# Feed-forward blocks of a hybrid transformer layer: where the norm's steps, the sums of x and the first loads stand

## The chip, the cores and the metric

One NeuronCore of a Trainium2 chip runs the whole program. Its engines work from their own queues, each in order: PE (TensorE, the matrix products; PEld is its loading of weights), DVE (VectorE), ACT (ScalarE), POOL (GpSimd) and SP, which here issues every DMA. They meet through semaphores. The metric is the device time of one execution in microseconds, as a median over runs.

## The reference

One layer over 512 tokens of width 1024: a feed-forward block, an attention mixer, a second feed-forward block, and a last norm. What the change touches is the first part of both feed-forward blocks.

```python
def rmsnorm(x, g):
    xf = x.astype(jnp.float32)
    y = xf * lax.rsqrt(jnp.mean(xf * xf, axis=-1, keepdims=True) + NORM_EPS)
    return (y * g.astype(jnp.float32)).astype(x.dtype)

def swiglu(x, w_in, w_out):
    gate, up = jnp.split(x @ w_in, 2, axis=-1)
    return (jax.nn.silu(gate) * up) @ w_out
...
        h = h + 0.5 * swiglu(rmsnorm(h, ffn1_norm[l]), ffn1_w_in[l], ffn1_w_out[l])
        h = h + hybrid_mixer(...)
        h = h + 0.5 * swiglu(rmsnorm(h, ffn2_norm[l]), ffn2_w_in[l], ffn2_w_out[l])
    return rmsnorm(h, final_norm)
```

`w_in` is 1024 x 5632, `w_out` 2816 x 1024.

## The kernel before

The state `h` lies transposed in SBUF: 8 blocks of 128 rows (the width) by 512 columns (the tokens). Every operand of a product is split into a high part (a rounded copy, made by ACT) and a low part (the rest, made by DVE), and a product is three matmuls: high by high, high by low, low by high (`mm3_steps`, L205 to L211, for 512 columns; `product`, L300 to L308, for 256). `parts` (L159 to L164) makes the two parts of a block of x times the norm's gain; the division by the root of the mean square is left out of the operands and multiplied into the results later (`gated`).

A feed-forward block is `ffn`. Its 22 column blocks of `w_in` (128 gates and 128 ups each) come in two kinds:

- the first three are **plain blocks**: two products of 24 matmuls of 512 columns each, one for the gates and one for the ups, six products in all. Their weights are read by SP into pieces (`load_next`, L110) and split by `to_parts` (L97 on ACT, L98 on DVE).
- the other 19 are computed in quarters by a scheme of seven products of 12 matmuls of 256 columns (a Strassen-like scheme), which uses sums of quarters of x (`sums_of_x`) and sums of quarters of the weights (`sums_of_w`, a loop that makes them one block ahead: L274, L278, L284 the sums on DVE, L276, L282, L288, L293 the high parts on ACT, L279, L285, L290, L295 the low parts on DVE). The seven products of a block are issued in the order B11, T1, T2, B21, B22, T3 and (after the next block's B11) T4. The products by `w_out` (`out_steps`) are pushed in between.

Before the scheme can start, the work that stands beside the plain blocks must be done: the **norm** (squares of h on ACT, L168 and L171, added up on DVE, L172; `rstd_col`: a product of the sum with ones on PE, L185, a root on ACT, L187, with a table load before it, a reciprocal on DVE, L189; `rstd_bc`: a product with the identity that spreads the result over the partitions, L196, copied by ACT, L200), the **sums of x** (scaled copies of h on ACT, L231; sums on DVE, L239, L240, L243, L244; their high parts on ACT, L247, and low parts on DVE, L248), the **gating** of the three plain blocks (L333, L337, L339 on DVE, the Silu on ACT, L335, the parts of the result, L326 and L328), and the first block's sums of w.

Order: the program is written as one stream, and generators (`side_step`) take a step of the sums of x or w at every second step of a product. A scheduler then lays each engine's queue down, and it can move an instruction ahead of its place in the text; it is fixed when the program is built. In the first feed-forward block the first two products run side by side while x and the weights are still loading (`two`, `steps`).

Tiles: `u` holds operands (32 buffers), `tmp` 128x512 scratch (10), `t8`/`t` raw weights (4 of 1 MB), `sm` the gains, `acc` the sum of squares; `mm`, `sc` and `pv` are PSUM banks (4, 3 and 1).

## Time and profile before

| | |
|---|---|
| median of 3 runs | 1008.36 us (1007.68 to 1011.56) |
| the profiled execution, its own time | 1003.63 us |
| its span | 1001.7 us |
| mean granted clock of TensorE in it | 0.991 |
| PE busy | 972.7 us (97%), 6196 matmuls |
| DVE, ACT busy | 802.5 us (80%), 511.4 us (51%) |
| DMA | 93.59 MB, mean 93 GB/s |

How to read it: the span is what the rows add up to; the time of the execution is 1.9 us longer. PE is busy nearly all the time, so the question is where it is not, and where it runs slowly. A row of the timeline gives the start, the duration, the engine, the line, the operation, what it writes and reads, and in brackets how long its engine had been idle and what it waited for. Matmuls overlap: the pitch from one start to the next tells the rate, not the duration of one.

### The profile page before, as it was taken

The page shows a single profiled execution, that of the slowest core. Times are in us where ns is not written, and L with a number is a line of the kernel's source. Part 1 is how long each engine was busy: PE and PEld are TensorE (multiplying, and loading weights), DVE is VectorE, ACT ScalarE, POOL GpSimd, SP SyncE. Part 2 cuts the span into 40 slices and gives each one's busy share as a digit, 9 for nine tenths or more (in the row PEclk, how much of TensorE's full clock was granted, in tenths as well). Part 3 has the DMA queues.
Part 4 walks back from the last instruction along what each step waited for, and adds up shares of the span by engine and source line. Part 5 has one row for each costly group of instructions (what it writes and reads, how often), then busy time and mean ns, then how long its engine had stood idle before and what let it go on. Part 6 is the DMA issues. An engine that isn't in the chain of part 4 may idle for free.

```text
span 1001.7 us, 15923 instructions
## 1 busy us (share of the span) xinstructions
PE 972.7 (97%) x6196; PEld 869.0 (87%) x6196; DVE 802.5 (80%) x1466; ACT 511.4 (51%) x1037; POOL 0.2 (0%) x4
## 2 busy tenths in 40 slices
PE   7899999999999999999999999979999999999996
PEld 5699999999999889888777888859999999999996
DVE  7699868788696675787899899789977878779665
ACT  8454344443444355554777786745534435344344
POOL 0000000000000000000000000000000000000000
PEclk9999999999999999999999999989999999999998
DMA  7233223122224313123311113114331323313112
GB/s 297 64 127 116 90 101 137 74 106 88 102 86 141 124 37 111 43 78 98 128 43 45 41 43 106 43 43 147 116 130 60 137 74 106 126 64 96 43 43 84
DMA packets 36506, 93.59 MB, mean 93 GB/s; under 512 B 4432, under 2 KB 8912, under 8 KB 36432
## 3 DMA queue, kind: packets, MB, share of 16 engines
q1 hardware_dynamic: 36432, 92.59, 26.8%
q8 instruction: 48, 0.79, 0.3%
q14 instruction: 26, 0.21, 0.1%
HBM read 88.87 MB, written 2.10 MB: 91 GB/s over the span
## 4 chain that ended last, share of the span: by engine, by line
PE 93%; DVE 3%; ACT 2%; issue 1%; DMA 1%; SPq 0%; DVEq 0%; ACTq 0%
PE mm L306 9%; PE mm L307 9%; PE mm L308 9%; PE sc L210 9%; PE sc L209 9%; PE sc L208 9%; PE mm L208 5%; PE mm L210 5%; PE mm L209 5%; PE sc L308 4%; PE sc L307 4%; PE sc L306 4%; PE mm L855 2%; PE pv L892 2%; PE pv L893 2%; PE mm L711 1%
## 5 line engine op out<-in xcount | busy, mean ns | idle before, releaser
L306 PE MATMUL mm<-u 128*128 128x256 f32 x760 | 214.9, 283 | 0.2 <-ACT u L282 0.2
L307 PE MATMUL mm<-u 128*128 128x256 f32 x760 | 215.0, 283 | 0.0
L308 PE MATMUL mm<-u 128*128 128x256 f32 x760 | 215.0, 283 | 0.0
L208 PE MATMUL sc<-u 128*128 128x512 f32 (+1 forms) x400 | 156.3, 391 | 7.7 <-ACT u L97 7.0
L210 PE MATMUL sc<-u 128*128 128x512 f32 (+1 forms) x400 | 155.0, 387 | 2.4 <-DVE u L98 2.4
L209 PE MATMUL sc<-u 128*128 128x512 f32 (+1 forms) x400 | 155.5, 389 | 0.0
L306 PEld LDWEIGHTS mm<-u 128*128 128x128 f32 x760 | 144.8, 191 | 7.6 <-DVE tmp L514 0.5
L307 PEld LDWEIGHTS mm<-u 128*128 128x128 f32 x760 | 145.1, 191 | 5.6
L308 PEld LDWEIGHTS mm<-u 128*128 128x128 f32 x760 | 145.0, 191 | 0.5
L208 PE MATMUL mm<-u 128*128 128x512 f32 (+1 forms) x248 | 98.8, 398 | 2.7 <-ACT u L97 2.7
L210 PE MATMUL mm<-u 128*128 128x512 f32 (+1 forms) x248 | 95.6, 386 | 0.1
L209 PE MATMUL mm<-u 128*128 128x512 f32 (+1 forms) x248 | 95.1, 383 | 0.0
L210 PEld LDWEIGHTS sc<-u 128*128 128x128 f32 x400 | 76.5, 191 | 20.3 <-DVE u L98 3.0
L306 PE MATMUL sc<-u 128*128 128x256 f32 x304 | 86.6, 285 | 5.2 <-ACT u L276 5.2
L208 PEld LDWEIGHTS sc<-u 128*128 128x128 f32 x400 | 77.3, 193 | 15.4 <-ACT u L97 7.4
L308 PE MATMUL sc<-u 128*128 128x256 f32 x304 | 86.6, 285 | 0.0
L307 PE MATMUL sc<-u 128*128 128x256 f32 x304 | 86.5, 285 | 0.0
L209 PEld LDWEIGHTS sc<-u 128*128 128x128 f32 x400 | 77.3, 193 | 6.5
L358 ACT CAST u<-tmp 128x512 fp32r<-128x512 f32 (+1 forms) x96 | 54.6, 582 | 43.9 <-PE sc L210 21.0
L381 DVE SCALAR_TENSOR_TENSOR h<-sc,h 128x512 f32<-128x512 f32 x85 | 58.4, 687 | 11.9 <-PE sc L210 11.8
L359 DVE TENSOR_TENSOR u<-tmp,u 128x512 fp32r<-128x512 f32 (+1 forms) x96 | 60.9, 641 | 8.5 <-ACT u L358 8.3
L306 PEld LDWEIGHTS sc<-u 128*128 128x128 f32 x304 | 58.5, 192 | 8.0 <-ACT u L276 5.4
(223 smaller groups left out, 1948.9 us busy)
## 6 DMA issues: line engine op xcount, KB each, us to landing
t<-in_f_wi_dram SPq DMA_DIRECT2D x86, 512.0 KB, 4.3
tmp<-in_f_wo_dram SPq DMA_DIRECT2D x80, 256.0 KB, 4.8
t<-in_wm_t_dram SPq DMA_DIRECT2D x13, 512.0 KB, 4.3
t<-in_cw_dram SPq DMA_DIRECT2D x8, 512.0 KB, 4.9
tmp<-in_f_wo_dram SPq DMA_DIRECT2D x16, 128.0 KB, 3.8
t<-in_wm_oa_dram SPq DMA_DIRECT2D x4, 512.0 KB, 3.9
out_dram<-tmp SPq DMA_DIRECT2D x8, 256.0 KB, 2.1
t<-in_wm_n_dram SPq DMA_DIRECT2D x4, 408.0 KB, 3.6
```

The lines of the kernel that those rows point to most:

```text
L208: PE.matmul(o, wh[:, c], xs[k][:, 0, :], start=s0, stop=False)
L209: PE.matmul(o, wh[:, c], xs[k][:, 1, :], start=False, stop=False)
L210: PE.matmul(o, wl[:, c], xs[k][:, 0, :], start=False, stop=s1)
L306: PE.matmul(o, w[0][:, c], x[k][0], start=new, stop=False, skip_group_check=not first)
L307: PE.matmul(o, w[0][:, c], x[k][1], start=False, stop=False, skip_group_check=not first)
L308: PE.matmul(o, w[1][:, c], x[k][0], start=False, stop=k == 3, skip_group_check=not first)
L358: A.copy(u[:, 0, :n], raw[:, :n])
L359: V.tensor_tensor(u[:, 1, :n], raw[:, :n], f(u[:, 0, :n]), op=ALU.subtract)
L381: V.scalar_tensor_tensor(h[:, i, :], o, 0.5, h[:, i, :], op0=ALU.mult, op1=ALU.add)
L855: PE.transpose(pt[:rows, r * P : (r + 1) * P], pl[r][:, cols], ident)
L892: PE.matmul(pv, v, u[:, 0, :], start=a, stop=False)
L893: PE.matmul(pv, v, u[:, 1, :], start=False, stop=b)
```

## The change

It has five parts, all in `ffn`'s plain blocks and in the program's first microseconds.

1. **First loads.** The table of gains is loaded first; the first two blocks of x come in one DMA (rows of 4 KB in place of 2 KB), and so does each of the first two pieces of weights, which were read in halves. Seven DMAs stand ahead of the identity's in place of ten; the rest of x follows in pairs of blocks as before.
2. **Products of ones.** Eight 128x128 products of a tile of ones (`wake`, L92) are issued on PE while these loads run. Nothing reads their result.
3. **Root's table.** ACT's first activation is a root (`late`, L88), so that the table for roots is loaded at the start; the load ahead of the norm's root in the first block is gone.
4. **Squares.** In the first block, the squares of h take their bias from `late`, which is written (as zero) after the last block of x is split. This orders them behind the splitting of x; four come after the first two products, the others at steps of the third.
5. **Norm's steps and sums of x.** In the first block the norm's product with ones stands after the third step of the fourth product, and the product with the identity after the second step of the fifth; in the second block after the fourth step of the first and the second step of the second. Before, the text had them between products. The sums of x are made in lots: scaled copies, sums, high parts and low parts of successive lots overlap by one, where before each lot was finished before the next was begun.

In the first two products the two are now advanced two steps at a time in turn, in place of one.

The diff, cut to its core:

```diff
--- before.py
+++ after.py
@@ -76,14 +76,20 @@
 
     h = sb.tile([P, KB, 512], F32, tag="h", name="h")
     sm = sb.tile([P, S_W], F32, tag="sm", name="sm")
-    nc.sync.dma_start(h[:, 0:1, :], xT[:, 0:1, :])
     nc.sync.dma_start(sm, small)
-
+    nc.sync.dma_start(h[:, 0:2, :], xT[:, 0:2, :])
+
+    epsc = sb.tile([P, 1], F32, tag="epsc", name="epsc")
+    V.memset(epsc, EPS)
     ones = sb.tile([P, P], F32, tag="ones", name="ones")
     V.memset(ones, 1.0)
-    epsc = sb.tile([P, 1], F32, tag="epsc", name="epsc")
-    V.memset(epsc, EPS)
-    A.copy(epsc, epsc)
+
+    late = sb.tile([P, 1], F32, tag="late", name="late")
+    A.activation(late, epsc, AF.Sqrt)
+
+    wake = ps("pv")
+    for _ in range(8):
+        PE.matmul(wake[:, :P], ones, ones, start=True, stop=True)
     ident = sb.tile([P, P], F32, tag="ident", name="ident")
     rowm = sb.tile([P, 1], F32, tag="rowm", name="rowm")
 
@@ -163,12 +169,12 @@
         A.activation(u[:, 0, :], h[:, k, :], AF.Copy, scale=gc)
         V.scalar_tensor_tensor(u[:, 1, :], h[:, k, :], gc, f(u[:, 0, :]), op0=ALU.mult, op1=ALU.subtract)
 
-    def squares(k, acc):
+    def squares(k, acc, zero=0.0):
         if k == 0:
-            A.activation(acc, h[:, k, :], AF.Square)
+            A.activation(acc, h[:, k, :], AF.Square, bias=zero)
         else:
             sq = tmp()
-            A.activation(sq, h[:, k, :], AF.Square)
+            A.activation(sq, h[:, k, :], AF.Square, bias=zero)
             V.tensor_tensor(acc, acc, sq, op=ALU.add)
 
     def feed(k, gcol, xs, acc):
@@ -222,33 +228,66 @@
 
     def sums_of_x(xs, gcol, XF):
 
-        xg = []
-        for u in range(4):
-            t = unit(F32)
-            xg.append(t)
-            for a in range(2):
-                k = 2 * u + a
-                A.activation(t[:, a, :], h[:, k, :], AF.Copy, scale=sm[:, gcol + k : gcol + k + 1])
-            yield
         t1, t2 = slice(0, 256), slice(256, 512)
-        for kp in range(2):
+        xg = [None] * 4
+
+        def scaled(*us):
+            for u in us:
+                t = xg[u] = unit(F32)
+                for a in range(2):
+                    k = 2 * u + a
+                    A.activation(t[:, a, :], h[:, k, :], AF.Copy, scale=sm[:, gcol + k : gcol + k + 1])
+
+        def sums(kp, n):
             a, b = xg[kp], xg[2 + kp]
-            for n in range(2):
-                s = flat(F32).rearrange("p (s k t) -> p s k t", s=2, k=2)
-                if n == 0:
-                    V.tensor_tensor(s[:, 0], a[:, :, t2], b[:, :, t2], op=ALU.add)
-                    V.tensor_tensor(s[:, 1], s[:, 0], a[:, :, t1], op=ALU.subtract)
-                    s2 = s[:, 1]
-                else:
-                    V.tensor_tensor(s[:, 0], a[:, :, t1], a[:, :, t2], op=ALU.subtract)
-                    V.tensor_tensor(s[:, 1], b[:, :, t1], s2, op=ALU.subtract)
-                yield
-                sh, sl = [flat().rearrange("p (s k t) -> p s k t", s=2, k=2) for _ in range(2)]
-                A.copy(sh, s)
-                V.tensor_tensor(sl, s, f(sh), op=ALU.subtract)
-                for m in range(2):
-                    XF["S", 2 * n + m + 1].extend((sh[:, m, k], sl[:, m, k]) for k in range(2))
-                yield
+            s = flat(F32).rearrange("p (s k t) -> p s k t", s=2, k=2)
+            if n == 0:
+                V.tensor_tensor(s[:, 0], a[:, :, t2], b[:, :, t2], op=ALU.add)
+                V.tensor_tensor(s[:, 1], s[:, 0], a[:, :, t1], op=ALU.subtract)
+                s2[kp] = s[:, 1]
+            else:
+                V.tensor_tensor(s[:, 0], a[:, :, t1], a[:, :, t2], op=ALU.subtract)
+                V.tensor_tensor(s[:, 1], b[:, :, t1], s2[kp], op=ALU.subtract)
+            return s
+
+        def high(s):
+            sh = flat().rearrange("p (s k t) -> p s k t", s=2, k=2)
+            A.copy(sh, s)
+            return sh
+
+        def low(s, sh, n):
+            sl = flat().rearrange("p (s k t) -> p s k t", s=2, k=2)
+            V.tensor_tensor(sl, s, f(sh), op=ALU.subtract)
+            for m in range(2):
+                XF["S", 2 * n + m + 1].extend((sh[:, m, k], sl[:, m, k]) for k in range(2))
+
+
+        s2 = [None] * 2
+        scaled(0)
+        yield
+        scaled(2)
+        yield
+        sa = sums(0, 0)
+        yield
+        scaled(1)
+        sb_ = sums(0, 1)
+        ha = high(sa)
+        yield
+        scaled(3)
+        low(sa, ha, 0)
+        yield
+        hb = high(sb_)
+        sc = sums(1, 0)
+        yield
+        low(sb_, hb, 1)
+        sd = sums(1, 1)
+        hc = high(sc)
+        yield
+        low(sc, hc, 0)
+        hd = high(sd)
+        yield
+        low(sd, hd, 1)
+        yield
         for name, ks, t in (("A11", 0, t1), ("A12", 4, t1), ("A22", 4, t2)):
             XF[name].extend((xs[k][:, 0, t], xs[k][:, 1, t]) for k in range(ks, ks + 4))
 
@@ -430,50 +469,57 @@
                     side.pop(0)
 
 
+        todo = state["squares"]
+        early = bool(todo)
+
+        rc_at, bc_at = ((3, 2), (4, 1)) if early else ((0, 3), (1, 1))
         side.append(sums_of_x(xs, gcol, XF))
-        for j in range(plain):
-            pz = []
-            if state["squares"] and j == 0:
-
-                two = [(split.pop(0), ps_any()) for _ in range(2)]
-                pz = [o for _, o in two]
-                steps = [mm3_steps(o, wh, wl, ALLK, xs, True, True) for (wh, wl), o in two]
-                for _ in ALLK:
+        done = []
+
+        def between(n, k):
+            nonlocal bc, rcol
+            if (n, k) == rc_at:
+                rcol = rstd_col(acc)
+            elif (n, k) == bc_at:
+                bc = rstd_bc(rcol)
+            elif k % 2 == 1:
+                if early and n == 2 and todo:
+                    squares(*todo.pop(0))
+                elif n > 0 or k > 3:
+                    side_step()
+
+        for n in range(2 * plain):
+            if early and n < 2:
+
+                if n == 0:
+                    two = [(split.pop(0), ps_any()) for _ in range(2)]
+                    steps = [mm3_steps(o, wh, wl, ALLK, xs, True, True) for (wh, wl), o in two]
+                    for _ in range(KB // 2):
+                        for g in steps:
+                            next(g)
+                            next(g)
                     for g in steps:
-                        next(g, None)
-                for g in steps:
-                    run(g)
-                split_next()
-                split_next()
-                for _ in range(4):
-                    squares(*state["squares"].pop(0))
-            for s in range(2 - len(pz)):
+                        run(g)
+                    split_next()
+                    split_next()
+                    for _ in range(4):
+                        squares(*todo.pop(0))
+                    done.extend(o for _, o in two)
+            else:
                 wh, wl = next_w(2)
                 o = ps_any()
-                for n, _ in enumerate(mm3_steps(o, wh, wl, ALLK, xs, True, True)):
-                    if n % 2 == 1:
-                        side_step()
-                pz.append(o)
-                if bc is None:
-                    todo = state["squares"]
-                    for _ in range(4):
-                        if todo:
-                            squares(*todo.pop(0))
-                    if not todo and rcol is None:
-                        rcol = rstd_col(acc)
-                    elif rcol is not None:
-                        bc = rstd_bc(rcol)
-                        while held:
-                            gated(*held.pop(0))
-            if bc is None:
-                held.append((j, *pz))
-            else:
-                gated(j, *pz)
-            if j == 0:
+                for k, _ in enumerate(mm3_steps(o, wh, wl, ALLK, xs, True, True)):
+                    between(n, k)
+                done.append(o)
+            if n == 1:
                 load_ahead()
-                for n in range(2):
-                    raws[plain + n] = load_raw(wi, plain + n)
+                for m in range(2):
+                    raws[plain + m] = load_raw(wi, plain + m)
                 side.append(sums_of_w(raws, wi, plain, WF))
+            if n % 2 == 1:
+                held.append((n // 2, *done[-2:]))
+            while bc is not None and held:
+                gated(*held.pop(0))
         side_step(20)
         outs.append(out_steps(0))
 
@@ -597,12 +643,9 @@
         to_parts(*first[j][1:], c)
 
     ca, cb = slice(0, 512), slice(512, 1024)
-    w_in(0, ca)
-    x_in(1, 1)
-    w_in(1, ca)
+    w_in(0, slice(0, 1024))
+    w_in(1, slice(0, 1024))
     x_in(2, 2)
-    w_in(0, cb)
-    w_in(1, cb)
     x_in(4, 2)
     x_in(6, 2)
     nc.sync.dma_start(ident, const[:, C_ID : C_ID + P])
@@ -616,7 +659,9 @@
     w_parts(1, cb)
     for k in range(4, KB):
         parts(k, S_G1, xs)
-    state["squares"] = [(k, acc) for k in range(KB)]
+
+    A.activation(late, f(xs[KB - 1][:, 0, 0:1]), AF.Copy, scale=0.0)
+    state["squares"] = [(k, acc, late) for k in range(KB)]
     xs, acc = ffn(xs, acc, f1_wi, f1_wo, NP1, S_GM)
```

How the queues move at three places. **ACT in the first feed-forward block**, from the last weights of the plain blocks on. Before (L97: high part of weights; L231: scaled copies; L187: the root; L247: high part of a lot of sums; L200: copy of the spread norm):

```order
L97 CAST u<-t_169 128x1024
L97 CAST u<-t_180 128x1024
L231 ACTIVATE u<-h,sm 128x512 x8
L187 ACT_TABLE_LOAD
L187 ACTIVATE rc<-pv,epsc 128x4
L97 CAST u<-t_180 128x1024
L247 CAST u<-u 128x1024
L200 COPY bc<-pv 128x512
L247 CAST u<-u 128x1024
L335 ACT_TABLE_LOAD
```

Now (L103, L239, L193, L255 and L206 are the same steps, L177 the squares, L374 the Silu):

```order
L177 ACTIVATE tmp<-h,late 128x512 x4
L103 CAST u<-t_188 128x1024
L239 ACTIVATE u<-h,sm 128x512 x5
L193 ACTIVATE rc<-pv,epsc 128x4
L239 ACTIVATE u<-h,sm 128x512
L255 CAST u<-u 128x1024
L239 ACTIVATE u<-h,sm 128x512 x2
L255 CAST u<-u 128x1024
L206 COPY bc<-pv 128x512
L255 CAST u<-u 128x1024
L374 ACT_TABLE_LOAD
L374 ACTIVATE tmp<-tmp 128x512
```

All six products' weights are now split ahead of the root, and three of the four lots' high parts stand ahead of the first Silu, where before two did.

**DVE at the same place.** Before (L98: low part of weights; L274, L278, L284: sums of w; L239, L240, L243, L244: sums of x; L248: low part of a lot):

```order
L172 TENSOR_TENSOR acc<-acc,tmp 128x512
L274 TENSOR_TENSOR t_379<-t_193 128x2x512
L278 TENSOR_TENSOR t_379<-t_193,t_379 128x512
L189 RECIPROCAL rcol<-rc 128x4
L284 TENSOR_TENSOR t_379<-t_193,t_379 128x512
L98 TENSOR_TENSOR u<-t_180,u 128x1024
L239 TENSOR_TENSOR u<-u 128x512
L240 TENSOR_TENSOR u<-u 128x512
L248 TENSOR_TENSOR u<-u 128x1024
L243 TENSOR_TENSOR u<-u 128x512
```

Now (L313, L317, L323: sums of w; L245, L246, L249, L250: sums of x; L260: low part of a lot):

```order
L104 TENSOR_TENSOR u<-t_188,u 128x1024
L178 TENSOR_TENSOR acc<-acc,tmp 128x512
L313 TENSOR_TENSOR t_399<-t_201 128x2x512
L245 TENSOR_TENSOR u<-u 128x512
L249 TENSOR_TENSOR u<-u 128x512
L195 RECIPROCAL rcol<-rc 128x4
L246 TENSOR_TENSOR u<-u 128x512
L317 TENSOR_TENSOR t_399<-t_201,t_399 128x512
L250 TENSOR_TENSOR u<-u 128x512
L260 TENSOR_TENSOR u<-u 128x1024
L323 TENSOR_TENSOR t_399<-t_201,t_399 128x512
L245 TENSOR_TENSOR u<-u 128x512
```

The last sum of squares now comes after the last low part of weights, and the reciprocal, which waits for the root, has most of the sums of x behind it.

**ACT in the second feed-forward block**, from the end of the mixer on. Before:

```order
L97 CAST u<-t_6336 128x1024
L231 ACTIVATE u<-h,sm 128x512 x8
L187 ACT_TABLE_LOAD
L187 ACTIVATE rc<-pv,epsc 128x4
L97 CAST u<-t_6543 128x1024
L200 COPY bc<-pv 128x512
L335 ACT_TABLE_LOAD
L335 ACTIVATE tmp<-tmp 128x512
L247 CAST u<-u 128x1024
L335 ACTIVATE tmp<-tmp 128x512
L247 CAST u<-u 128x1024
L326 CAST u<-tmp 128x512
```

Now (L365: high part of a gated block):

```order
L103 CAST u<-t_6344 128x1024
L239 ACTIVATE u<-h,sm 128x512
L193 ACT_TABLE_LOAD
L193 ACTIVATE rc<-pv,epsc 128x4
L239 ACTIVATE u<-h,sm 128x512 x3
L103 CAST u<-t_6551 128x1024
L206 COPY bc<-pv 128x512
L239 ACTIVATE u<-h,sm 128x512 x2
L255 CAST u<-u 128x1024
L239 ACTIVATE u<-h,sm 128x512 x2
L374 ACT_TABLE_LOAD
L374 ACTIVATE tmp<-tmp 128x512
```

The root and its table load now stand behind one scaled copy in place of eight, and the next weights behind four. On PE the norm's product with the identity (L196, now L202) moves ahead by 19 matmuls there.

## The prediction

> **What bounds the kernel now.** The page first: the chain that ended last, by engine.
>
> ```profile
> PE 93%; DVE 3%; ACT 2%; issue 1%; DMA 1%; SPq 0%; DVEq 0%; ACTq 0%
> ```
>
> PE is on 93% of the chain of waits, and the change takes no product away. So it can win only where PE stands idle, or runs at a low clock, beside the edited code. The stretches of the plain blocks and what follows them (length, then PE, PEld, DVE, ACT, POOL busy, granted clock, DMA share, GB/s):
>
> ```profile
> 21.24:45.28 24.04, 24.03 (x115) 20.00 (x113) 16.92 (x25) 13.21 (x18) 0.00 (x0) 1.00 0.25 80
> 45.28:57.31 12.03, 6.70 (x38) 6.32 (x39) 11.01 (x14) 7.75 (x12) 0.00 (x0) 0.72 0.08 17
> 57.31:70.00 12.69, 12.69 (x88) 11.75 (x87) 12.60 (x22) 5.58 (x10) 0.00 (x0) 1.00 0.59 218
> 640.00:676.30 36.30, 30.07 (x123) 23.71 (x122) 26.02 (x33) 19.93 (x26) 0.00 (x0) 0.91 0.18 59
> ```
>
> PE is full during the first block's plain products and loses half of the 12 us behind them, with the clock at 0.72; in the second block it loses 6.2 of 36.3 us, at 0.91. The waits of PE in these stretches (total, times, longest):
>
> ```profile
> PE sc L306 <- ACT u L276: 5.2, 1, 5.2
> PE mm L208 <- ACT u L97: 2.4, 1, 2.4
> PE sc L210 <- DVE u L98: 2.4, 1, 2.4
> PE sc L208 <- ACT u L97: 1.4, 1, 1.4
> ```
>
> The first is at the start of the scheme in block one, the others at the fifth and sixth plain products of block two. The front of the program comes next, in PE's timeline.
>
> ```profile
> 5.59 0.80 PE L208 MATMUL sc<-u 128*128 128x512 f32 x1 [5.59 <-ACT u L97]
> 9.00 0.80 PE L208 MATMUL mm<-u 128*128 128x512 f32 x1 [0.23 <-ACT u L97]
> 12.69 0.63 PE L208 MATMUL sc<-u 128*128 128x512 f32 x1
> 13.94 0.40 PE L209 MATMUL mm<-u 128*128 128x512 f32 x1
> 21.23 0.39 PE L208 MATMUL sc<-u 128*128 128x512 f32 x1
> 26.68 0.95 PE L185 MATMUL pv<-ones,acc 128*128 128x1 f32 x8
> 33.07 1.05 PE L196 MATMUL pv<-ident,rcol 128*128 128x128 f32 x8
> 33.88 0.48 PE L208 MATMUL mm<-u 128*128 128x512 f32 x1
> 44.88 0.40 PE L485 MATMUL mm<-u 128*128 128x256 f32 x2
> 50.46 0.58 PE L306 MATMUL sc<-u 128*128 128x256 f32 x1 [5.19 <-ACT u L276]
> ```
>
> From 9.00 on PE is fed without a break, but matmuls last 0.63 us until 12.69 and 0.40 after 13.94: a cold clock for some 4 us. The row at 21.23 is the first behind 48 matmuls, so the third product starts there. From 21.23 to 26.68 are 24 matmuls: 0.227 us each, the warm pitch.
>
> **The change, part by part. The front.** Loads first. Two stretches of one microsecond, from 6 and from 9 us on, settle how much rows of 4 KB can bring:
>
> ```profile
> DMA packets 70, 0.23 MB, mean 227 GB/s; under 512 B 5, under 2 KB 5, under 8 KB 70
> DMA packets 160, 0.43 MB, mean 430 GB/s; under 512 B 15, under 2 KB 15, under 8 KB 160
> ```
>
> The slow one has packets of 3.3 KB on average (0.23 MB over 70), the fast one of 2.7 KB. What is slow is the time, not the row. By "DMA: Bandwidth & Descriptors" in the Trainium skill (Specifications), rows of 512 bytes or more already run at line rate, which agrees with these two rows; by it this edit wins nothing.
>
> PE is fully fed once two blocks of x and the first pieces of two weights are in and split. Before, these were 1.1 MB (half pieces), now 1.6 MB (whole ones). In the old order the load that completed the first 1.6 MB was the second pair of x, and ACT waited for it until 9.15:
>
> ```profile
> 9.15 1.33 ACT L163 ACTIVATE u<-h,sm 128x512 fp32r<-128x512 f32 x2 [0.20 <-DMA h<-in_xT_dram]
> ```
>
> With half a microsecond of ACT for the weight that lands last, the full feed comes at 9.8 (0.8 late) at the old rate. At 430 GB/s from the start (1.6 MB in 3.7 us, beginning at 2 us and landing one behind) ACT's eight steps of 0.5 to 0.6 us are the limit, and it comes near 8.3 (0.7 early).
>
> The ones: four products of 128 columns cost 0.81 us (33.07 to 33.88), so eight take 1.6 us warm and 3.2 us cold, from about 1 us to 4.3 us. They hold nothing up, since the first product waited until 5.59 and cannot start earlier now. If they left the clock warm, the 4 cold microseconds would hold twice the work: up to 1.9 us won. But 4 us of full feed were needed at 9.00, and some 3 us of idle follow. The Trainium skill (TensorE: Matmul & The Clock Gate, Part 1) has the gate open only after a busy window of about 3.4 us and close after an idle one; by it the wake is as good as lost, the side I take. Ends for the front: -0.8 and +2.6 us; I take **0**, so the third product starts at S = 21.2 again.
>
> **Block one, the stop of 5.2 us.** PE reaches the norm's product with ones after 33 matmuls of 0.227: S+7.5. Durations for the rest:
>
> ```profile
> 17.96 1.98 ACT L97 CAST u<-t 128x1024 fp32r<-128x1024 f32 x2
> 19.84 5.01 ACT L231 ACTIVATE u<-h,sm 128x512 f32<-128x512 f32 x8
> 27.71 1.28 ACT L187 ACT_TABLE_LOAD   x1 [2.85 <-PE pv L185]
> 29.00 0.26 ACT L187 ACTIVATE rc<-pv,epsc 128x4 f32<-128x4 f32 x1
> 29.30 0.18 DVE L189 RECIPROCAL rcol<-rc 128x4 f32<-128x4 f32 x1 [4.84 <-ACT rc L187]
> 19.63 2.36 DVE L98 TENSOR_TENSOR u<-t,u 128x1024 fp32r<-128x1024 f32 x2
> 627.56 1.88 DVE L1085 TENSOR_TENSOR h<-mm,h 128x512 f32<-128x512 f32 x3
> ```
>
> Pitches: ACT 0.95 for 1024 columns, 0.62 for a scaled copy; DVE 1.13 and 0.60 (1.88 less 0.69, halved).
>
> First, does the sum of squares arrive? On DVE the two parts' work up to the last sum is 8 splits of x, 4 halves and 4 whole weights and 7 additions; behind the last splits of x (14.5) and ACT's squares and casts it ends near 23.5 to 24.7, PE asks at 28.7: cover 4 us. Behind that, DVE makes a sum of w and two sums of x and then **stands at the reciprocal**, with the sums of x queued behind it. Product 0.95, root 0.26, reciprocal 0.18 put it at S+8.9 (the table load of 1.28 is gone). From there to the low part of T1, DVE's queue holds 20 operations of 0.60, four of 1.13, 0.65 of waiting for the first Silu (ACT loads its table behind the third high part) and the low part itself: 12.0+4.5+0.65+1.2 = 18.4, so S+27.3.
>
> PE: 96 matmuls and two norm products of 0.8 put the end of the plain blocks at S+23.6 (before: 44.88+0.40 = 45.28, that is S+24.0). ACT's high part of B11 is ready at S+23.6, of T1 at S+24.6, its low part at S+25.0; T1's low part at S+27.3. PE waits some 0.1, 0.65, 0.35 and 0.95 us and has B11, T1 and T2 (36 matmuls at 0.12) done at S+29.9. Lost: 6.3-4.3 = 2.0 us. Before, from 45.28 to 57.31, the same 36 and two of `w_out` (4.8 us) took 12.03: 7.2 lost, idle and cold clock together. Gain **5.2 us**. If DVE's 18.4 were all slack it would be 7.2; if it waits twice as long for Silu and high parts as I count (3 us more) and PE cools, 1.
>
> DVE is as good as full just behind (12.60 of 12.69), so does it catch up? The low part of T1 of the next block and PE's first use of it:
>
> ```profile
> 59.61 1.22 DVE L285 TENSOR_TENSOR u<-t,u 128x1024 fp32r<-128x1024 f32 x1
> 69.56 0.28 PE L306 MATMUL mm<-u 128*128 128x256 f32 x1
> ```
>
> 8.7 us of slack between 60.83 and 69.56; a PE that is 5 us early against a DVE 4 to 6 us early leaves it whole.
>
> **Block two, 6.2 us of stops.** The root sat behind eight scaled copies, and each weight behind it.
>
> ```profile
> 638.29 5.01 ACT L231 ACTIVATE u<-h,sm 128x512 f32<-128x512 f32 x8
> 644.78 1.04 ACT L97 CAST u<-t 128x1024 fp32r<-128x1024 f32 x1
> 654.55 0.39 PE L210 MATMUL sc<-u 128*128 128x512 f32 x1
> 658.12 1.22 DVE L98 TENSOR_TENSOR u<-t,u 128x1024 fp32r<-128x1024 f32 x1
> 659.98 0.63 PE L208 MATMUL sc<-u 128*128 128x512 f32 x1
> 660.41 0.63 PE L209 MATMUL sc<-u 128*128 128x512 f32 x1
> 668.80 1.03 ACT L97 CAST u<-t 128x1024 fp32r<-128x1024 f32 x1
> 669.86 1.23 DVE L98 TENSOR_TENSOR u<-t,u 128x1024 fp32r<-128x1024 f32 x1 [0.56 <-ACT u L97]
> ```
>
> The fifth product could start at 654.78; it began late, and after the stops ran at a pitch of 0.43 (659.98 to 660.41: cold).
>
> Now: one scaled copy, table load and root to 640.5, three copies to 642.3, the fourth product's weights to 643.3 (before: 644.78+1.04). The product with the identity, at 642.0 on PE, waits for nothing. DVE: low part to 644.5, three sums to 646.3; ACT: first lot's high part to 647.4, two copies, Silu's table to 650.0, Silu 650.6; DVE's product 651.3, its high part 652.0, then the **fifth product's weights**: high 652.9, low 654.2. PE wants them at 654.8 and 655.2: in time, with 1.0 us of cover. The sixth's low part stands on DVE behind a sum (0.6), a low part (655.9), three sums (657.7), a low part (658.9), a sum of w (660.0) and a low part (661.1): ready at 662.3. PE is there at 660.7 and waits 1.6 us; I count no cooling for so short a stop. The sixth ends at 667.4; before, 676.3. Gain 8.9; I take **8.6**. Without the cover of 1.0, each microsecond is one lost.
>
> The other edits: the squares' bias costs ACT nothing it did not pay, and the two writes of `late` are activations of one column. SP issues three DMAs less ahead of the later weights, which are loaded long before they are used.
>
> **Sum**: 0+5.2+8.6 = 13.8 us off the profiled execution's 1003.63 (span 1001.7 plus 1.9): 989.8. That execution is 4.7 us under the median; the same step from 1008.36 gives 994.5, rounded to **994**.
>
> **The rivals.** *Half only*: the reciprocal in DVE's queue eats block one's gain, or the sixth product's weights block two's (both engines' walks are exact to a microsecond or two, over 20 operations). For it: the cover of 1.0 us, and DVE already full at 57 us. Against: both need two more waits than I find. One gain of 5 to 8 remains: 1001. *Warm start*: the ones open the gate and it stays open, or the loads run at 430 GB/s: 2.6 more, 992. For it: the ones last almost the window; against: 3 us of idle, and the row at 227 GB/s. *As it was*: the scheduler's queues trade one wait for another of the same size: 1008; against it, the table load gone and weights 1.5 us earlier in block two. *Slower*: PE, in order, stands at the norm's product with ones, whose last sum now has the fourth whole weight's low part ahead of it on DVE and so its load on SP. Each microsecond beyond the cover of 4 us stops PE, then cools it; it turns the kernel slower from a load 4+14 = 18 us late, and at 24 us late gives 1014. The weights' loads of the front, issue to landing, before:
>
> ```profile
> t<-in_f_wi_dram SPq DMA_DIRECT2D x10, 512.0 KB, 8.0
> ```
>
> A median of 8.0 us with the queue as full: 26 is unlikely.
>
> **Chances**: forecast 0.56, half only 0.19, warm start 0.11, as it was 0.08, slower 0.06. Within 0.5% (5 us, what a measurement here can just tell) are 1003.3 to 1013.4: faster 0.85 (the first three, less a little of half only), same 0.09, slower 0.06. Range 987 to 1003: the lower end is the warm start with all of block one's 7.2, the upper takes in half only.
>
> **What would show it.** After the plain blocks no wait of PE above 1.5 us, clock 1.00 there; DVE idle about 3 us before the reciprocal; in block two one wait of PE, 1 to 2 us, for L104 at the sixth product, none at the fifth. Matmuls of ones at the cold pitch, and cold ones again at 9 us. Wrong if PE waits over 3 us for L315 or L324, or the third product starts later than 23 us.

## The result, and the profile after

The changed kernel takes **994.58 us** (median; 994.02 to 994.93) against 1008.02 for the kernel before in the same comparison: a ratio of 0.988, interval 0.986 to 0.990: faster by 1.2%, clear of the spread. The forecast was 994. The kernel before spreads far more (1004.76 to 1011.56 here; medians of 1004.8, 1006.5 and 1005.0 in the three comparisons below), and its profiled execution took 1003.63. So the gain is 9.1 us between the two profiled executions, 10 to 13 between medians, where the sum said 13.8.

Lines have moved: the split of the weights is L103 and L104 now (L97, L98), the norm's product, root and reciprocal L191, L193, L195, the sums of w with their parts L313 to L334, plain products L214 to L216, scheme products L345 to L347, gating L372 to L378 and its parts L365 and L367, the split of `w_out` L397 and L398. L551 (before L505) is DVE's sum that the product of B22 adds to: it needs T2 and ACT's copy of T1, L548.

The page after, span and chain by engine:

```profile
span 992.8 us, 15952 instructions
PE 89%; DVE 6%; ACT 3%; DMA 1%; issue 1%; SPq 0%; DVEq 0%; ACTq 0%
```

The stretches that answer to those of before (length, then PE, PEld, DVE, ACT, POOL busy, granted clock, DMA share, GB/s): block one's plain products from the third on, the scheme's first three products, block two from the root to the end of the sixth product, and what follows it.

```profile
20.63:44.26 23.63, 23.63 (x113) 19.80 (x112) 20.21 (x31) 15.98 (x24) 0.00 (x0) 1.00 0.22 77
44.26:51.06 6.80, 5.83 (x39) 4.83 (x38) 6.50 (x9) 4.78 (x9) 0.00 (x0) 1.00 0.08 23
634.59:662.19 27.60, 26.46 (x122) 21.89 (x121) 22.70 (x29) 18.85 (x25) 0.00 (x0) 1.00 0.23 77
662.19:675.48 13.29, 10.54 (x63) 9.30 (x61) 11.31 (x19) 7.07 (x13) 0.00 (x0) 0.87 0.45 150
```

Block one is cured: 6.80 us with a full clock, where 12.03 at 0.72 stood. Block two is full up to the end of the sixth product. Then comes a stretch that nobody had asked about, with 2.75 us of idle PE and the clock at 0.87. PE's timeline at these places:

```profile
1.07 3.78 PE L92 MATMUL pv<-ones 128*128 128x128 f32 x16 [1.07 <-DVE ones L85]
7.48 0.50 PE L214 MATMUL sc<-u 128*128 128x512 f32 x1 [2.62 <-ACT u L103]
8.62 0.79 PE L214 MATMUL sc<-u 128*128 128x512 f32 x1
12.19 0.39 PE L216 MATMUL mm<-u 128*128 128x512 f32 x1
45.62 0.39 PE L345 MATMUL mm<-u 128*128 128x256 f32 x1 [0.44 <-ACT u L321]
47.99 0.38 PE L345 MATMUL mm<-u 128*128 128x256 f32 x1 [0.45 <-ACT mm L541]
657.07 0.50 PE L216 MATMUL mm<-u 128*128 128x512 f32 x1 [1.14 <-DVE u L104]
670.00 0.38 PE L345 MATMUL mm<-u 128*128 128x256 f32 x1 [2.14 <-DVE mm L551]
671.23 0.79 PE L214 MATMUL sc<-u 128*128 128x512 f32 x1 [0.61 <-ACT u L397]
672.25 0.63 PE L216 MATMUL sc<-u 128*128 128x512 f32 x1
674.56 0.39 PE L216 MATMUL sc<-u 128*128 128x512 f32 x1
```

The last five rows are block two: the predicted wait at the sixth product, then one for L551, one for `w_out`, and matmuls of 0.63 us until 674. Why L551 was late stands in the queues. DVE first, with the reciprocal and T1's low part of block one ahead:

```profile
29.38 0.18 DVE L195 RECIPROCAL rcol<-rc 128x4 f32<-128x4 f32 x1 [2.35 <-ACT rc L193]
47.29 1.22 DVE L324 TENSOR_TENSOR u<-t,u 128x1024 fp32r<-128x1024 f32 x1
666.94 0.69 DVE L378 TENSOR_TENSOR tmp<-tmp 128x512 f32<-128x512 f32 x1
667.54 0.68 DVE L323 TENSOR_TENSOR t<-t,t 128x512 f32<-128x512 f32 x1
668.31 0.69 DVE L367 TENSOR_TENSOR u<-tmp,u 128x512 fp32r<-128x512 f32 x1
668.92 0.69 DVE L318 TENSOR_TENSOR u<-t,u 128x512 fp32r<-128x512 f32 x1
669.52 0.43 DVE L551 TENSOR_TENSOR mm<-mm,tmp 128x256 f32<-128x256 f32 x1
```

and ACT:

```profile
667.66 0.62 ACT L365 CAST u<-tmp 128x512 fp32r<-128x512 f32 x1 [2.65 <-DVE tmp L378]
668.70 0.36 ACT L548 COPY tmp<-mm 128x256 f32<-128x256 f32 x1
670.77 0.78 ACT L397 CAST u<-tmp 128x256 fp32r<-128x256 f32 x2 [1.70 <-DMA tmp<-in_f_wo_dram]
```

In PE's timeline T1 is done near 664.9 and T2 near 666.4; B21 then fills PE until 667.9. But ACT stood 2.65 us for the third plain block's gating (L378), with the copy of T1 behind it, and DVE had gating and the next block's sums of w ahead of L551. The load of `w_out` landed no sooner than 670.8, so PE had nothing else. SP had issued it late, behind a load of w that waited for a buffer:

```profile
657.04 9.01 SPq L297 DMA_DIRECT2D t<-in_f_wi_dram  x4
666.10 3.36 SPq L388 DMA_DIRECT2D tmp<-in_f_wo_dram  x7
```

### The profile page after: what moved, and what is told of

Read it like the earlier page. It is cut to its first block, busy times and chain, and to the rows that moved or that the text cites. A ratio compares the mean times of both kernels' runs of the same rounds, so it can differ in the third digit from the quotient of the medians.

```text
span 992.8 us, 15952 instructions
## 1 busy us (share of the span) xinstructions
PE 973.4 (98%) x6212; PEld 870.1 (88%) x6212; DVE 801.8 (81%) x1466; ACT 510.8 (51%) x1037; POOL 0.2 (0%) x4
## 4 chain that ended last, share of the span: by engine, by line
PE 89%; DVE 6%; ACT 3%; DMA 1%; issue 1%; SPq 0%; DVEq 0%; ACTq 0%
PE mm L347 9%; PE mm L346 9%; PE mm L345 9%; PE sc L214 8%; PE sc L216 8%; PE sc L215 8%; PE mm L214 4%; PE mm L216 4%; PE mm L215 4%; PE sc L346 4%; PE sc L347 4%; PE sc L345 4%; PE mm L900 2%; PE pv L937 2%; PE pv L938 2%; PE mm L756 1%
## 5 line engine op out<-in xcount | busy, mean ns | idle before, releaser
L345 PE MATMUL mm<-u 128*128 128x256 f32 x760 | 214.7, 283 | 3.0 <-DVE mm L551 2.1
L347 PE MATMUL mm<-u 128*128 128x256 f32 x760 | 214.5, 283 | 0.1
L214 PE MATMUL sc<-u 128*128 128x512 f32 (+1 forms) x400 | 155.3, 388 | 3.2 <-ACT u L103 2.6
L216 PE MATMUL sc<-u 128*128 128x512 f32 (+1 forms) x400 | 153.9, 385 | 0.0
L345 PEld LDWEIGHTS mm<-u 128*128 128x128 f32 x760 | 144.5, 190 | 10.7 <-DVE mm L551 2.3
L347 PEld LDWEIGHTS mm<-u 128*128 128x128 f32 x760 | 144.6, 190 | 0.9 <-DVE u L324 0.3
L214 PE MATMUL mm<-u 128*128 128x512 f32 (+1 forms) x248 | 98.4, 397 | 0.0
L216 PE MATMUL mm<-u 128*128 128x512 f32 (+1 forms) x248 | 95.1, 384 | 1.1 <-DVE u L104 1.1
L216 PEld LDWEIGHTS sc<-u 128*128 128x128 f32 x400 | 75.7, 189 | 17.8 <-DVE u L398 1.8
L347 PE MATMUL sc<-u 128*128 128x256 f32 x304 | 86.0, 283 | 0.0
L214 PEld LDWEIGHTS sc<-u 128*128 128x128 f32 x400 | 76.6, 192 | 10.7 <-ACT u L103 2.9
L345 PE MATMUL sc<-u 128*128 128x256 f32 x304 | 85.8, 282 | 0.0
L397 ACT CAST u<-tmp 128x512 fp32r<-128x512 f32 (+1 forms) x96 | 54.8, 583 | 48.0 <-PE sc L216 21.7
L398 DVE TENSOR_TENSOR u<-tmp,u 128x512 fp32r<-128x512 f32 (+1 forms) x96 | 61.0, 641 | 9.5 <-ACT u L397 9.2
L420 DVE SCALAR_TENSOR_TENSOR h<-sc,h 128x512 f32<-128x512 f32 x85 | 58.3, 686 | 12.2 <-PE sc L216 12.2
L345 PEld LDWEIGHTS sc<-u 128*128 128x128 f32 x304 | 57.9, 190 | 2.9 <-ACT u L315 0.2
```

The costliest lines, as they stand in the source:

```text
L214: PE.matmul(o, wh[:, c], xs[k][:, 0, :], start=s0, stop=False)
L216: PE.matmul(o, wl[:, c], xs[k][:, 0, :], start=False, stop=s1)
L345: PE.matmul(o, w[0][:, c], x[k][0], start=new, stop=False, skip_group_check=not first)
L347: PE.matmul(o, w[1][:, c], x[k][0], start=False, stop=k == 3, skip_group_check=not first)
L397: A.copy(u[:, 0, :n], raw[:, :n])
L398: V.tensor_tensor(u[:, 1, :n], raw[:, :n], f(u[:, 0, :n]), op=ALU.subtract)
```

## Experiments

Three milestones tell where each kernel wins: the norm's product in block two (all that is ahead of it: front, block one, mixer), the start of the program's last products, and the time between the two (block two and the rest). All are from PE's timelines; the median is of four runs (eight for the kernel before again).

| kernel | median | norm, block two | last products | from one to the other |
|---|---|---|---|---|
| before, first profile | 1008.02 | 638.59 | 994.67 | 356.08 |
| before, second profile | 1005.09 | 641.97 | 998.46 | 356.49 |
| changed | 994.58 | 633.18 | 985.24 | 352.06 |
| without the ones | 995.41 | 633.29 | 985.28 | 351.99 |
| sixteen ones | 994.05 | 631.98 | 985.18 | 353.20 |
| old first loads | 997.29 | 634.76 | 985.28 | 350.52 |
| new loads cut to 2 KB rows | 994.68 | 634.50 | 986.34 | 351.84 |
| gating on GpSimd | 1000.46 | 636.71 | 991.93 | 355.22 |
| old sums of x | 996.38 | 640.40 | 988.09 | 347.69 |
| old norm in block two | 991.46 | 633.44 | 981.85 | 348.41 |
| gating later | 990.09 | 633.80 | 981.40 | 347.60 |
| gating later, early `w_out` | 990.43 | 632.57 | 980.62 | 348.05 |
| the same, sixteen ones | 989.11 | 631.56 | 979.62 | 348.06 |
| the same, old norm in block two | 986.48 | 631.76 | 977.73 | 345.97 |

The rows come from four comparisons, and the changed kernel was run in the first alone, so differences of a microsecond between medians say little; the milestones say more, with a scatter of their own. Five kernels have the changed kernel's block two and differ only in the first microseconds (changed, without the ones, sixteen ones, old first loads, 2 KB rows): from one milestone to the other they take 350.52 to 353.20.

**The front: without the ones.**

```diff
-    wake = ps("pv")
-    for _ in range(8):
-        PE.matmul(wake[:, :P], ones, ones, start=True, stop=True)
```

> The changed kernel without the eight products of ones at the start (nothing reads them, so no part of the result is left out). In the changed kernel the products of ones ran from 1.07 to 3.78 us, the first four real products that followed, from 7.48 on, took 0.40 to 0.51 us each, and from 8.6 on 0.63 to 0.79. Theory of the prediction (the wake is as good as lost): the first products run cold, at 0.63 us and more, from 7.5 to about 11.5; the third product starts at 20.6 to 21.3 (20.62 in the changed kernel); time as the changed kernel's 994.6 to within 0.7 us. Rival (the warm start): the ones are what won the 0.6 us by which the third product moved ahead (21.23 to 20.62), since four or five products at 0.45 instead of 0.68 are 1 us: third product at 21.2 to 21.6, time 995.2 to 995.6.

The first product began at 7.28, matmuls were slow from there to 12.2, and block one's norm product came at 28.22 (28.10 with the ones). In the six kernels of the table that share the changed kernel's front (the changed one, gating on GpSimd, old sums, old norm in block two, the first two with the later gating) it came between 27.44 and 28.65, so the 0.1 is nothing. The median is 0.8 above the changed kernel's, inside this run's spread of 3.8. Eight products of ones are as good as lost, as predicted.

**Sixteen for eight** (`range(8)` becomes `range(16)`).

> The changed kernel with sixteen products of ones for eight (nothing reads them). The eight end at 3.78 us and TensorE then stands 2.6 us until its first real product at 7.48. If it is this stand that lost the clock (the four products that ran at 0.45 us, then 0.7 until 11.9), sixteen products, eight of which at the quick rate of about 0.2 to 0.25 us, end at 5.5 to 6.5 us, the stand is 1 to 2 us, and the clock holds: no product over 0.55 us after 7.5 us, the third product 20.6 - 1.5 = 19.1, time 993.1. Theory of the prediction (the wake is as good as lost, since what sets the start is the loads and the rounding behind them): the 1.5 us are taken back by waits for rounded parts, which come no sooner than about 0.65 us apart: third product still 20.6, time 994.6 within 0.7 us.

PE's timeline of this kernel:

```profile
1.07 6.14 PE L92 MATMUL pv<-ones 128*128 128x128 f32 x32 [1.07 <-DVE ones L85]
7.18 0.50 PE L214 MATMUL sc<-u 128*128 128x512 f32 x1
668.78 0.39 PE L345 MATMUL mm<-u 128*128 128x256 f32 x1 [2.11 <-DVE mm L551]
670.97 0.50 PE L214 MATMUL sc<-u 128*128 128x512 f32 x1 [1.57 <-ACT u L397]
```

The ones now reach to the first product, and no slow matmul followed until 671.5. The rounded parts hardly held it back (one wait of 0.53 us): block one's norm product came at 26.95, 1.15 us sooner, and so did everything to 668.8. There the gain ended: `w_out`'s load came no sooner, its wait grew from 0.61 to 1.57, and the last products start at the same instant. The two other kernels with sixteen have block one's norm product at 26.43 and 26.64, sooner than any of the six with eight.

**The loads.** Twice: the old loads in their old order, and then the new order with each of the first transfers cut into two of 2 KB rows:

```diff
-    nc.sync.dma_start(h[:, 0:2, :], xT[:, 0:2, :])
+    for q in range(2):
+        nc.sync.dma_start(h[:, q : q + 1, :], xT[:, q : q + 1, :])
...
-    w_in(0, slice(0, 1024))
-    w_in(1, slice(0, 1024))
+    w_in(0, ca)
+    w_in(0, cb)
+    w_in(1, ca)
+    w_in(1, cb)
```

> The changed kernel with the first loads of the kernel before in their old order: rows of 2 KB for the first blocks of x and w instead of 4 KB, the rest of the change kept. The changed kernel's DMA moved 287, 344, 389, 401 and 426 GB/s in the microseconds from 3 to 8, the kernel before 249 to 277. Theory of the prediction (what is slow is the time after the start, not the row): the rate from 3 to 8 us stays over 340 GB/s with the old rows, the third product starts at 20.6 within 0.3, time 994.6 within 0.7 us. Rival (the row, or the order of the transfers, sets the rate): from 3 to 8 us the rate falls back to 250 to 280 GB/s, the products after the second wait for rounded parts, the third product starts at 21.2 or later, and the time is 995.2 to 996.5.

> The changed kernel with the first loads cut in two: the same bytes in the same order, but x's first two blocks as two transfers of 2 KB rows and each of w's first two pieces as two transfers of 2 KB rows. With the old loads in their old order (2 KB rows, x and w in turn) the DMA had fallen to 191 and 170 GB/s in the microseconds from 4 to 6, against 344 and 389. If it is the row (the rival of the prediction): the rate from 4 to 7 us stays at 170 to 300 GB/s, the first products come as late as with the old loads, time 995.5 to 998. If it is the order and what arrives together: the rate is 340 GB/s and more from 4 us on, time 993.5 to 995.5. Theory of the prediction (the row wins nothing) asks for the second.

The microsecond from 5 to 6 us, in the changed kernel and in the one with the cut rows:

```profile
DMA packets 108, 0.39 MB, mean 389 GB/s; under 512 B 13, under 2 KB 13, under 8 KB 108
```

```profile
DMA packets 139, 0.24 MB, mean 244 GB/s; under 512 B 20, under 2 KB 20, under 8 KB 139
```

With the old loads the rate from 3 to 8 us was 170 to 322 GB/s, with the cut rows 244 to 346, with the changed kernel's 287 to 426. All ten profiles with rows of 4 KB moved 365 to 397 GB/s in this microsecond. Same bytes, same order, same time after the start: it is the size of the row (or the number of transfers, which doubles with it), not the time. What it is worth here is little: the first product began at 8.05 for 7.48, block one's norm product at 28.80 (27.44 to 28.65 in the six kernels above), and the median is the same. The old order costs more in the median (997.3, spread 994.6 to 998.8), yet its profiled execution ended with the changed kernel's. In it the first product began at 5.01, and the third no later than in the changed kernel (20.70 for 20.62). Then a new stop stands in block one:

```profile
45.93 0.39 PE L345 MATMUL sc<-u 128*128 128x256 f32 x1 [1.17 <-ACT u L315]
```

It brings block two's norm product 1.6 us later. Behind block two's stops (2.10 and 0.45 us) the clock stayed full this time, where the changed kernel's was lost; that gave 1.5 us back. This was the shortest of the four executions, and the other three, 2.7 to 4.2 us longer, have no trace, so the rest of the price stays open.

**The sums of x as they were**, in both blocks, the norm at its new places.

```diff
-    def sums_of_x(xs, gcol, XF):      # one lot ahead
+    def sums_of_x(xs, gcol, XF):      # that of the kernel before
```

> The changed kernel with the old sums of x in both blocks (all four scaled lots first, then sum, cast and low part in turn, none ahead of another); the norm's steps stay at their new places. In the changed kernel block one's plain products end at 44.3 us, B11, T1 and T2 follow with waits of 0.44 and 0.45 us only, and T2 is done at 51.1; the norm product of the mixer runs at 365.94 (371.35 before). Theory of the prediction (block one's 5.2 us come from the sums in lots one ahead): with the old sums TensorE stands 4 to 5.5 us behind block one's plain products for a rounded part of the sums, as it did for 5.19 before, and the mixer's norm product comes at 370 to 371.5; block two gains or loses up to 1 us more; time 998.5 to 1000.5. Rival (the place of the norm freed the gap, not the lots): the stand is under 2 us, time 994.5 to 996.5.

PE's waits in block one and in block two:

```profile
51.41 0.58 PE L312 MATMUL sc<-u 128*128 128x256 f32 x1 [6.29 <-ACT u L282]
671.02 0.39 PE L314 MATMUL mm<-u 128*128 128x256 f32 x1 [0.65 <-DVE u L291]
```

Block one's stop is back: the norm's new place alone does not cure it, the lots one ahead are needed. Whether they suffice with block one's norm at its old place was not run. The time was better than expected for a reason that no theory had: in block two the old sums with the new norm leave no wait above 0.65 us at all. From the norm's product to the end it takes 347.69, 8.4 less than the kernel before. This is the 8.6 that the prediction gave to the norm's place, and the changed kernel, with the new sums beside it, keeps 4.0 of it (2.9 to 5.6 by the five kernels above). Not only the sums differ, for the scheduler has laid SP's queue otherwise too: five loads of `w_out` stand ahead of the load of w that waits, where in the changed kernel all seven stand behind it.

```profile
663.56 4.09 SPq L355 DMA_DIRECT2D tmp<-in_f_wo_dram  x5
```

**The norm of block two where it was**, the new sums kept.

```diff
-        rc_at, bc_at = ((3, 2), (4, 1)) if early else ((0, 3), (1, 1))
+        rc_at, bc_at = ((3, 2), (4, 1)) if early else ((1, 0), (2, 0))
```

> The changed kernel with block two's norm steps back at their old places among the products (the new sums of x and block one stay). The changed kernel's block two waits 1.14 us at the sixth product, then 2.14, 0.61 and about 1.6 us of slow products behind it; the kernel before waited 1.37, 2.35 and 2.44 us at the fourth to the sixth and had 13 slow products. Theory of the prediction (the place of the norm is worth 8.6 us): the waits at the fourth to sixth product come back, the sixth ends 8 to 9 us later (670 to 671 instead of 662.2), time 1001 to 1003.5. Theory now (5 us of these were given back behind the sixth, in a stop for L551 that the earlier end only uncovered): the sixth ends 8 to 9 us later, the stop for L551 is gone or under 0.5 us, no slow products behind it, time 997.5 to 999. Rival (the new lots, not the norm's place, freed block two): the sixth ends at 662 to 664 as now, time 994 to 996.

Nearest to the rival, and beyond it: 991.46, 3.1 us under the changed kernel. No wait at any plain product; the only one in block two is

```profile
668.76 0.50 PE L214 MATMUL sc<-u 128*128 128x512 f32 x1 [2.06 <-ACT u L397]
```

and no slow matmuls follow. So either of the two edits frees block two by itself (8.4 and 7.7 us); they remove the same stops, and together they win 4.0. Why the new sums do better with the norm at its old place was not followed up.

**The gating on GpSimd**, to empty DVE's queue ahead of L551.

```diff
-            V.tensor_tensor(gg, zu, sg, op=ALU.mult)
-            run(put_g(j, gg))
+            nc.gpsimd.tensor_tensor(gg, zu, sg, op=ALU.mult)
+            run(put_g(j, gg, nc.gpsimd))
```

> The changed kernel with the plain blocks' gating product and low part (the last step behind the Silu, L378 and L367) on GpSimd instead of VectorE; same arithmetic. After the change block two's sixth product waits 1.14 us for L104's low part and the product of B22 waits 2.14 us for L551, both VectorE; then 0.61 us for L397 and about 1.6 us of slow products (0.63 instead of 0.23 us). Theory now: the cause of the 2.14 us is VectorE's queue, in which L551 stands behind the next block's sums of w and the gating steps of the plain blocks; with those steps on GpSimd L551 runs at once, the wait and the slow products behind it go, and 3 to 5 us are won: 989.5 to 991.5. Rival one (the sums of w are late whatever stands ahead of them, since their load or their PSUM operand comes late): the wait stays over 1.5 us, time 994 to 995. Rival two (GpSimd's steps are slow and the products that read them now wait): one elementwise step of 128 x 512 takes over 2 us on GpSimd, the products of w_out wait for it, time 995 or over.

1000.46, where 989.5 to 991.5 was expected. The wait for L551 grew to 3.94 us, and block one got three stops (1.35, 0.56 and 1.56 us; block two's norm product comes 3.5 us later). Rows of GpSimd, ACT and DVE:

```profile
671.97 1.59 POOL L378 TENSOR_TENSOR tmp<-tmp 128x512 f32<-128x512 f32 x1 [1.29 <-issue]
673.59 0.62 ACT L365 CAST u<-tmp 128x512 fp32r<-128x512 f32 x1 [2.79 <-POOL tmp L378]
667.21 2.32 DVE L334 TENSOR_TENSOR u<-t,u 128x1024 fp32r<-128x1024 f32 x1
674.76 1.34 DVE L318 TENSOR_TENSOR u<-t,u 128x512 fp32r<-128x512 f32 x1 [2.33 <-ACT u L315]
```

GpSimd's product takes 1.6 us on the mean (DVE's 0.69), ACT stands for it with the copy of T1 behind, DVE stands 2.33 us for ACT's L315, which is behind it too, and some DVE steps that run beside GpSimd's take longer (2.32 for 1.22). DVE had less to do and was later: by these rows ACT's queue mattered as much as DVE's.

**The gating later.** The third plain block's result is read by nobody before the second group of `w_out`, so its gating can be written behind T2 and L551; first alone, then with the first two loads of `w_out` written ahead of the last loads of w, then with sixteen ones as well, and last with the norm of block two at its old places.

```diff
-            while bc is not None and held:
+            while bc is not None and held and not (gnext is None and held[0][0] == plain - 1):
                 gated(*held.pop(0))
...
             piece_of(j, p)
+            if (j, p) == (plain, 6):
+                while held:
+                    gated(*held.pop(0))
```

> The changed kernel with the later gating of the third plain block alone; the loads of w_out stay where they are. With both edits the time was 990.4 and no stop was left behind the sixth product. Theory now (two causes in a row: first VectorE's queue ahead of L551, then the load of w_out, which lands at 670.5 to 670.8 whatever the engines do): the later gating alone only moves the stop from L551 to the load, since L398 stands ahead of L551 in VectorE's queue; a stop of 1.5 to 3 us for L397 or L551 stays and the clock may go with it: 992.5 to 995. Rival (the gating alone is the cause): 990 to 991.5.

> The changed kernel with two edits in block two alone: the third plain block's gating (L372 to L378 and the parts of its result, which nothing reads before the second group of w_out) is written behind the product T2 and L551 of the first scheme block instead of ahead of them; and the first two loads of w_out are issued ahead of the last loads of w, which wait on SyncE's queue for a free buffer. In the changed kernel VectorE runs L376, L317, L378, L323 and L367 (each 0.6 us) between 665.7 and 669 ahead of L551, and the w_out load lands at 670.8. Theory now (the 2.14 us stop is VectorE's and ScalarE's queue ahead of L551, the 0.61 us stop the load): L551 runs 1.5 to 2.5 us sooner, the stop falls under 0.8 us, the one for w_out is gone, no slow products follow, time 990 to 991.5. Rival (the clock is lost at this place even behind a short stop): the stops fall but the slow products stay, time 991.5 to 993. Rival (the loads ahead take the DMA's time from w): a wait for w's parts opens at the sixth or later, time 994 or over.

> The kernel of the run with the later gating in block two, with sixteen products of ones at the start for eight (nothing reads them). With sixteen the clock held from 7 us on and every milestone up to 668 us came 1.2 us sooner (T2's product for L541 at 46.84 for 47.99, the product of B22 at 668.78 for 670.00), and then the load of w_out, which came no sooner, took it back. Theory now: without that load in the way the 1.2 us stay; time 1.0 to 1.4 us under the run without the eight more products, 988.8 to 990.3. Rival (something else behind block two is fixed in time): no difference, within 0.4 us.

> The kernel with the later gating, the early loads of w_out and sixteen products of ones, and in addition block two's norm steps back at their old places. That kernel has one wait left in block two, 1.15 us for L104's low part at the sixth product; with the norm at its old places and the new sums that wait was gone. Theory now (with the new sums of x the new place of the norm costs block two 1.1 us at the sixth product and wins nothing there): 0.8 to 1.3 us under that kernel's 989.1, 987.8 to 988.3. Rival (VectorE is full from the norm to L551 either way, so the wait comes back at L551): the same time within 0.5 us, 988.6 to 989.6.

Alone it takes 990.09, with the loads 990.43: the second edit adds nothing. SP's queue in the kernel with the first edit alone says why:

```profile
658.56 1.80 SPq L388 DMA_DIRECT2D tmp<-in_f_wo_dram  x4
```

The scheduler, with the gating gone, has put four loads of `w_out` ahead of the load of w that waits for a buffer (in the changed kernel all seven stood behind it, at 666.10). So the queue ahead of L551 and the place of those loads changed together, and their shares are not separated by a run. In the changed kernel nothing on ACT or DVE between the sixth product's end and L551 reads `w_out`, so the stop of 2.14 us is the queues' and only that of 0.61 the load's. Both stops are gone, and the only wait left in block two is the 1.18 at the sixth product. Sixteen ones then keep their gain: 1.3 us less. The norm back at its old places takes the last wait away, and 2.6 us between medians of two comparisons, 1.9 between the profiled spans (986.6 and 984.7), more than the 0.8 to 1.3 expected; PE waits nowhere in block two. **986.48 us**, 0.981 of the kernel before (0.979 to 0.984), is the best version found, 8.1 under the changed kernel's median (measured in another comparison).

**The kernel before, once more**, for its spread.

> The kernel before once more, unchanged, for a second profile. Its times so far run from 1002.9 to 1011.6, the changed kernel's from 994.0 to 994.9. Theory now (the stops are the same in every execution, but the slow products behind them last until an instant that does not keep to the program, so that a stop costs more or less by when it falls): the same waits as in the first profile to within 0.2 us, but the stretches of slow products (5.6 to 13.3 us, 45.3 to 57.3 and 659.4 to 665.3 in the first profile) begin or end elsewhere, and the difference of the two spans is half the difference of their lengths. Rival (loads or waits differ from execution to execution): waits that differ by over 0.5 us.

PE's timeline of this second execution:

```profile
474.19 1.63 PE L711 MATMUL mm<-u,t 128*128 128x62 f32 x12 [0.78 <-DMA t<-in_cw_dram]
662.78 0.50 PE L210 MATMUL sc<-u 128*128 128x512 f32 x1 [2.36 <-DVE u L98]
663.97 0.63 PE L208 MATMUL sc<-u 128*128 128x512 f32 x1
667.22 0.40 PE L210 MATMUL sc<-u 128*128 128x512 f32 x1
673.98 0.63 PE L209 MATMUL mm<-u 128*128 128x512 f32 x1
677.34 0.40 PE L208 MATMUL mm<-u 128*128 128x512 f32 x1
```

The waits of the feed-forward blocks behind the first products repeat to 0.02 us (2.36 for 2.35, 2.44 twice). The slow stretches do not: in the first profile PE was slow from the stop at 659.4 on until 665.3 and full at the sixth; here it resumed at full rate, turned slow 1.2 us later for 3.3 us, and again behind the sixth. A further stretch stands at 477.8 to 482.8, which the first profile lacks. Slow stretches add up to 23.8 us here and 17.7 there; half of the difference, 3.1, and one new wait of 0.78 for a load make 3.9 of the 4.2 us between the spans (1005.9 and 1001.7). Most of it lies in the mixer, which took 2.9 us longer with the new wait and the slow stretch behind it; from block two's norm to the last products the two differ by 0.4. So both explanations hold, and whether the new wait brought on that stretch is not shown.

The granted clock, read in windows of 0.05 us, shows what the slow stretches keep to. In this profile it changes, up to the last products, at 49.2, 56.0, 475.9, 482.7, 663.6, 667.0, 673.9 and 677.3 us: 0, 2, 125, 127, 180, 181, 183 and 184 times 3.413 us after the first change. In the first profile it changes at 47.5, 54.3, 658.5 and 665.3 us, 0, 2, 179 and 181 times. By the Trainium skill (TensorE: Matmul & The Clock Gate, Part 1) the window on whose activity the clock is set runs free and lasts about 3.4 us; the trace agrees.

## Why the prediction was right, and where it was not

The time came out right; the sum behind it did not.

- **Block one, 5.2**: right. The squares ended at 24.7 (23.5 to 24.7), DVE stood 2.35 us at the reciprocal (3), T1's low part came at 48.5 (47.9), the stretch of 6.80 us holds 36 matmuls at 0.12 and a pair at 0.4, so 2.1 were lost for the 2.0 of the sum (waits of 0.44 and 0.45, and shorter gaps), and the three products ended at 51.06 (S+29.9, 50.5). Front and block one together brought the norm of block two from 638.59 to 633.18: 5.4 us. Which of the two edits does it was left open; the run with the old sums shows that the lots are needed, and whether they suffice without the norm's new place is not shown.
- **The front, 0**: 0.6, within its ends, and within the scatter: the third product started at 21.23 and 20.81 in the two profiles of the kernel before, at 19.95 to 21.17 in the six with this front. One reason for it was wrong. "What is slow is the time, not the row" fell: 2 KB rows at the same place moved 244 GB/s where 4 KB rows moved 389. By the Trainium skill (DMA: Bandwidth & Descriptors, Specifications) rows of 512 bytes or more run at line rate; the measurement differs, and decides. It was cheap: the third product started at 21.32 with 2 KB rows, for 20.62. The ones were as good as lost, as said, though not always cold: the first three matmuls (an expectation says four) took 0.40 to 0.51 before the clock fell. That sixteen would be worth 1.2 us was not seen.
- **Block two, 8.6**: here the step failed. Up to the sixth product all of it held: root at 634.91 (635.1 with 5.4 off), no wait at the fifth, one of 1.14 at the sixth (1.6), the sixth done at 662.19 (662.0). But "the sixth ends at 667.4; before, 676.3" was taken for the gain, as though all behind it were as before. For block one DVE's slack behind the stop was looked up; for block two it was not. There stood L551 behind the gating and sums of w on DVE, its operand behind ACT's wait for that gating, `w_out`'s load behind a waiting load on SP. Stops of 2.14 and 0.61 us and seven matmuls of twice the pitch (1.4) are 4.2 of the 4.6 given back: 4.0 are left of 8.6.
- **The sum**: 13.8 off 1003.63 would have been 989.8; the profiled execution took 994.49. The 994 came from taking the same step from the median of 1008.36, which lay 2 to 4 us above the kernel's later medians. So a good part of the agreement is luck. (The step from it was rounded down: 1008.36 less 13.8 is 994.56.) The sum's true term is 5.4 + 4.0.
- **Signs**: full clock behind the plain blocks, one wait at the sixth, slow matmuls at 9 us, all seen; "no wait of PE above 1.5 us" held behind block one and not behind block two. Of the rivals, "half only" described what the trace shows of block two, by another mechanism than either of its two.

## What to carry to other kernels

When a stop goes, walk on in every queue to the next operand that PE needs, on the new clock, until the slack is back; the end of the product that waited is no place to stop. Two edits that remove the same stop do not add, and may collide in the queues that both fill: run each without the other. A step whose result is read late should not stand ahead of one that is read at once, in the same engine's queue.

## What was not expected of the hardware

- A slow stretch begins and ends at instants that do not belong to the program: in the two profiles of the kernel before, the changes of the granted clock lie whole numbers of 3.413 us apart. So the same stop may cost a stretch or nothing: behind L551 and `w_out`'s load (2.14 and 0.61 us) the changed kernel ran slow from 671.2 to 674.2, the one with the old first loads (2.10 and 0.45 us) did not.
- Four runs of the best version lie within 0.5 us, those of the kernel before between 1002.9 and 1011.6. That fewer stops are the reason is not shown: with sixteen ones and both stops four runs lie within 0.4 us too, without ones and with the same stops within 3.8.
- The clock stayed full when sixteen products of ones reached to within 0.7 us of the first real product (three profiles), and was lost, at once or after 1.1 us, behind stands of 2.4 to 3.2 us (seven profiles). With the old loads eight reached to within 0.2 us of it, and the clock was lost behind the stands of 1.2 and 1.1 us that followed.
- A VectorE step of 1.22 us took 2.32 beside a GpSimd step, and two of 0.68 took 1.18 and 1.34; three others beside GpSimd steps kept their time.
